# Hybrid decoder layer on one core: where the MLP gate is applied, where the last residual is added, and how w2's preparation and w_out's halves are ordered

## Chip, core and metric

The kernel runs as one program on one core of a Trainium2 chip. The metric is the device time of one execution, in microseconds (us), shown as the median of three runs. The engines are named as in the profile: PE (TensorE matmul), DVE (VectorE), ACT (ScalarE), POOL (GpSimd) and SP (SyncE, which issues the DMAs).

## The reference

One decoder layer with 2048 tokens of width 1024 in float32. What matters here is the second half:

```python
y = jnp.concatenate([a, r], axis=-1) @ w_out[l]
x = layer_norm(ALPHA * x + gt1 * y, ln1_g[l], ln1_b[l])

h = x * (1.0 + sc2) + sh2
f = jnp.square(jax.nn.relu(h @ w_ff1[l])) @ w_ff2[l]
x = layer_norm(ALPHA * x + gt2 * f, ln2_g[l], ln2_b[l])
```

`a` and `r` are the results of multi-head latent attention and of retention. `gt1` and `gt2` are rows of 1024 numbers, the same for all tokens, that are computed from the condition vector `c`. `w_ff1` is 1024 x 4096, `w_ff2` is 4096 x 1024, `w_out` is 1024 x 1024. Since `gt2` scales columns, it can be multiplied into `f` or into the columns of `w_ff2`.

## The kernel before

All products are made of float32 operands split into a high part and a rest: `split` (L122 to L129) rounds on ACT (L126) and subtracts on DVE or POOL (L129), and `mm3` (L131 to L134) issues three matmuls. So each operand costs one ACT and one DVE pass before PE can use it, and the third matmul, which needs the low part of the weights, is the one at L134.

The program runs in stages. Up to about 1076 us of the span it does the conditioning, the input projections, retention and attention. Then follow:

- **w_out** (L925 to L1007, about 1076 to 1280 us): token tiles in pairs, 16 in all, in four groups of four (`border`). The columns of w_out are worked in two halves, n=0 and n=1. Raw rows of w_out are multiplied by `gt1` (L954: POOL for half 0, DVE for half 1) and split into `wo`, which lies in the pools `wo0` and `wo1`. For each pair the residual part `axl` is prepared (ACT L985, POOL L986 with the row `ag`, DVE L987 with the row `ab`); `ag` and `ab` are loaded and scaled on POOL first (L959). The sum with the product is normalised (L1000, L1001), stored to `z_d`, transposed on PE (L965), scaled on ACT (L967, `h2f`) and stored as the MLP's input.
- **FFN up** (L1060 to L1185, about 1280 to 1995 us): two halves of the tokens. In each, 16 channels of w_ff1 are worked in pairs with a Winograd-Strassen scheme of seven products per channel (`up`, `prod`), each product being 12 matmuls of 128x512. The weights of a product are combined on POOL (L1080), split into `w1h` (ACT) and `w1l` (DVE), and the seven combinations of the input (`hh`, `hl`) come from `split_h`. The results are squared ReLUs that are stored to `g_d`.
- Beside that, `prep` and `work` prepare w_ff2: 16 units, eight in each half, each with a 1 MB load `w2r` and then seven pieces. A piece subtracts (DVE L1140), splits into one of two buffers `w2s` (ACT L126, DVE L129) and stores to `wt_d` (L1143). The loop at L1151 to L1185 takes pieces from the generator `todo` after each product, at a pace that `slots` and `want` set. In the last quarter of the units (s=3) the raw rows are multiplied by `gt2` first (L1134, two multiplies of 128x1024 a unit).
- **FFN down** (`down`, L1251 to L1334, about 1997 to 2649 us): two halves of the tokens, four steps s each. A step has seven products of 48 matmuls (P1, P5, P6, P3, then P7, P2, P4; in s=3 P2 stands before P7). The operands `gP..h` and `gP..l` are split from `a` (loaded from `g_d`, combined at L1272), the weights `wP` are loaded from `wt_d`. After each product its PSUM tiles are added to `acc` in SBUF (L1304). At s=2, `gate` (L1215) multiplies each quarter of `acc` by `gt2` once that quarter's last product of the step is added, 16 multiplies of 128x512 in each half: what the first three steps add carries no gate yet. At s=3, `residual` (L1220) loads four pieces `zt` from `z_d`, scales them on POOL (L1226, L1227) and adds them on DVE (L1229), for one quarter after each of P1, P5, P6 and P3. `finish` (L1231) normalises and stores.

The order of the instructions on each engine is not written out by hand. The framework's scheduler sets it from the order and the dependences of the program as written; `tc.issue_after(i)` makes it place what is issued inside the block behind instruction `i`. `load_rows` (L1206) loads the four rows that `residual` and `finish` use, after step s=1 of half 0.

The pools of one stage reuse the memory of pools that were closed before, so which tiles a new stage overwrites depends on the order in which the pools were opened.

## Time and profile before

| what | value |
|---|---|
| median of 3 runs | 2664.97 us (2663.29 to 2665.64) |
| profiled execution | 2665.75 us, span 2663.9 us |
| busy PE | 2453.7 us, 92% of the span |
| busy DVE | 1816.5 us, 68% |
| busy ACT | 1202.8 us, 45% |
| busy POOL | 1160.7 us, 44% |

A row of the timeline is: start, duration, engine, line, operation, output<-inputs, shape, count, and in brackets how long the engine had been idle and what released it. A row of the windows is: the stretch and its length, then the busy time of each engine with the number of instructions, the granted TensorE clock as a share of full speed, the DMA engines' busy share, GB/s. A group of instructions ends with busy time, mean duration in ns, idle time before it and its releaser. A row of the waits gives the engine and instruction that waited, what it waited for, and total us, how often, and the longest. Durations of neighbouring instructions on an engine overlap by a few hundredths to a few tenths of a us.

### The profile page before, as it was taken

To read this page: it belongs to the slowest core of one execution; us is meant where nothing else is said; L and a number is where in the kernel's file an instruction comes from. 1 tells how busy PE (TensorE), PEld (TensorE's weight loads), DVE (VectorE), ACT (ScalarE), POOL (GpSimd) and SP (SyncE) were. 2 spreads that over 40 slices of the span, in tenths; PEclk is the share of its full clock that TensorE was granted. 3 is DMA by queue.
4 is the path that set the end of the run, shared out by engine and by line. 5 is a ranking of instruction groups with operands and counts; after the bars stand their busy time and mean duration, and the time that the engine had idled before them with its cause. 6 is when DMAs were issued, how large, how long until landed. Compare 5 with 4: busy or idle time off the path is not lost.

```text
span 2663.9 us, 34047 instructions
## 1 busy us (share of the span) xinstructions
PE 2453.7 (92%) x11668; PEld 2020.8 (76%) x11668; DVE 1816.5 (68%) x2927; ACT 1202.8 (45%) x2349; POOL 1160.7 (44%) x1087
## 2 busy tenths in 40 slices
PE   6999999989999999699799999889999999899996
PEld 5877778877787878588576787767778887778874
DVE  8757675566767676644767757877544568965698
ACT  5653222257777777333546555456552211232111
POOL 4323546557888988433303236323310004730056
PEclk9999999989999999799899999999999999999998
DMA  9466341020202021555488833877538676776553
GB/s 325 144 216 205 112 136 39 32 78 25 64 17 64 22 60 40 177 177 202 154 283 295 285 124 119 274 261 272 193 137 320 243 277 233 282 291 245 207 209 138
DMA packets 205773, 464.71 MB, mean 174 GB/s; under 512 B 18840, under 2 KB 53016, under 8 KB 191264
## 3 DMA queue, kind: packets, MB, share of 16 engines
q1 hardware_dynamic: 205600, 462.54, 49.9%
q8 instruction: 92, 1.51, 0.2%
q14 instruction: 81, 0.66, 0.1%
HBM read 313.30 MB, written 149.17 MB: 174 GB/s over the span
## 4 chain that ended last, share of the span: by engine, by line
PE 58%; DVE 16%; DMA 13%; issue 5%; ACT 5%; POOL 3%; SPq 1%; DVEq 0%; ACTq 0%; POOLq 0%
DMA wt_d<-w2s 6%; PE t L835 3%; PE d_W L134 3%; PE d_W L132 3%; PE d_W L133 3%; DMA wad<-in_w_ada 2%; PE psY L133 2%; PE psY L134 2%; PE psY L132 2%; PE pj L134 2%; PE pj L132 2%; PE o L826 2%; PE pj L133 2%; PE o L828 2%; PE s L132 2%
## 5 line engine op out<-in xcount | busy, mean ns | idle before, releaser
L1080 POOL TENSOR_TENSOR w<-w,w 128x512 f32<-128x512 f32 x112 | 166.8, 1495 | 385.5 <-DMA w<-in_w_ff 225.4
L129 DVE TENSOR_TENSOR w1l_P<-w,w1h_P 128x512 fp32r<-128x512 f32 x224 | 202.6, 907 | 76.0 <-ACT w1h_P L126 75.3
L807 ACT ACTIVATE p<-s,nm 128x512 f32<-128x512 f32 (+3 forms) x320 | 196.6, 627 | 42.6 <-DVE nm L804 39.1
L802 DVE TENSOR_REDUCE mx<-s 128x1 f32<-128x512 f32 (+3 forms) x288 | 175.2, 621 | 56.5 <-PE s L134 53.7
L1226 POOL TENSOR_TENSOR zt<-zt,ag 128x512 f32<-128x512 f32 x32 | 52.5, 1652 | 307.2 <-DMA zt<-z_d 307.2
L851 POOL TENSOR_TENSOR tl<-tf,th 128x512 fp32r<-128x512 f32 x144 | 183.6, 1287 | 1.7
L835 PE MATMUL t<-ident,p 128*128 128x128 f32 x1088 | 165.5, 277 | 7.3 <-DVE tl L129 3.2
L126 ACT ACTIVATE w1h_P<-w 128x512 fp32r<-128x512 f32 x224 | 136.9, 620 | 74.1 <-PE u_Y L133 23.2
L835 PEld LDWEIGHTS t<-ident,p 128*128 128x128 f32 x1088 | 130.9, 142 | 32.7 <-ACT tf L846 6.4
L133 PE MATMUL pj<-wbl,hhb 128*128 128x512 f32 x384 | 151.4, 395 | 0.7 <-DVE wbl L129 0.7
L132 PE MATMUL pj<-wbh,hhb 128*128 128x512 f32 x384 | 150.7, 395 | 0.9 <-ACT wbh L126 0.6
L134 PE MATMUL pj<-wbh,hlb 128*128 128x512 f32 x384 | 151.4, 395 | 0.0
L129 DVE TENSOR_TENSOR w2s<-w2r,w2s 128x512 fp32r<-128x512 f32 x112 | 95.8, 858 | 73.7 <-ACT w2s L126 73.4
L132 PE MATMUL s<-kt,qt 96*128 96x512 f32 (+3 forms) x320 | 129.5, 405 | 12.3 <-ACT p L807 10.2
L126 ACT ACTIVATE w2s<-w2r 128x512 fp32r<-128x512 f32 x112 | 70.3, 629 | 150.3 <-DMA wt_d<-w2s 137.2
L826 PE MATMUL o<-th,v 128*128 128x512 f32 (+2 forms) x320 | 123.6, 391 | 5.0 <-DVE osum L862 4.2
L828 PE MATMUL o<-tl,v 128*128 128x512 f32 (+2 forms) x320 | 124.5, 398 | 3.3 <-DVE tl L129 1.8
L133 PE MATMUL s<-kt,qt 96*128 96x512 f32 (+3 forms) x320 | 119.9, 375 | 3.7 <-DVE kt L129 3.7
L134 PE MATMUL s<-kt,qt 96*128 96x512 f32 (+3 forms) x320 | 119.7, 375 | 0.0
L132 PE MATMUL psY<-wo_h,mh 128*128 128x512 f32 x256 | 101.4, 402 | 18.8 <-ACT wo_h L126 18.3
L134 PE MATMUL u_Z<-hh_P,w1l_P 128*128 128x512 f32 x256 | 102.9, 402 | 14.9 <-DVE w1l_P L129 14.9
L134 PE MATMUL u_X<-hh_P,w1l_P 128*128 128x512 f32 x256 | 102.8, 402 | 10.8 <-DVE w1l_P L129 10.6
(376 smaller groups left out, 7739.5 us busy)
## 6 DMA issues: line engine op xcount, KB each, us to landing
wP<-wt_d SPq DMA_DIRECT2D x112, 1024.0 KB, 5.0
wt_d<-w2s SPq DMA_DIRECT2D x112, 512.0 KB, 4.2
w<-in_w_ff SPq DMA_DIRECT2D x128, 256.0 KB, 3.5
a<-g_d SPq DMA_DIRECT2D x32, 1024.0 KB, 6.0
g_d<-v SPq DMA_DIRECT2D x96, 256.0 KB, 3.5
wad<-in_w_ada SPq DMA_DIRECT2D x64, 256.0 KB, 2.9
w2r<-in_w_ff SPq DMA_DIRECT2D x16, 1024.0 KB, 5.5
x<-in_x SPq DMA_DIRECT2D x16, 512.0 KB, 8.1
```

The lines of the kernel that those rows point to most:

```text
L126: A.activation(hi, x, AF.Copy)
L129: lo_eng.tensor_tensor(lo, x, hi.bitcast(F32), op=OP.subtract)
L132: T.matmul(ps, sh, mh, start=start, stop=False, skip_group_check=more)
L133: T.matmul(ps, sh, ml, start=False, stop=False, skip_group_check=more)
L134: T.matmul(ps, sl, mh, start=False, stop=stop, skip_group_check=more)
L802: V.tensor_reduce(mx[:, j:j + 1], ps[:, :n], op=OP.max, axis=AX.X)
L807: A.activation(pt[:, :m], b[:, :m], AF.Exp, bias=nm, accum_out=rs[:, qi, j:j + 1])
L826: T.matmul(po[:, cs], w, th[:, cs], start=(done == 0), stop=False)
L828: T.matmul(po[:, cs], w, tl[:, cs], start=False, stop=(done == nk))
L835: T.transpose(tp[:, qi * P:(qi + 1) * P], pts[h, 4 * qb + qi, kb // 4][1][:, kb % 4 * P:(kb % 4 + 1) * P], ident)
L851: (V if mode == "C" else G).tensor_tensor(tl[:, cs], tf[:, cs], th[:, cs].bitcast(F32), op=OP.subtract)
L1080: (V if half == 0 and c < W1V else G).tensor_tensor(src, *sub, op=op)
```

## The change

1. Every unit of w2 is multiplied by `gt2` before it is split (it was one unit in four). The two multiplies of a unit are now two pieces of their own, so a unit has nine pieces and `want` is 72 in each half. `gate` with its 32 multiplies of `acc` is gone.
2. `residual` adds one quarter in each step, after P6 (it was all four quarters in s=3). `load_rows` is called in the first step of half 0, after P5.
3. The instruction that makes a product's low part `w1l` is kept in the list `lows`, and each piece of w2 is issued behind the latest of them.
4. The pools `wo0` and `wo1` change places, and the last pair of token tiles works half n=1 of w_out before n=0.

```diff
--- before.py
+++ after.py
@@ -58,7 +58,7 @@
 WTB = 21
 WMS = "GV"
 WLS = "VV"
-RES = dict(P1=(0, 1), P5=(1, 1), P6=(0, 0), P3=(1, 0))
+RES = (0, 0), (1, 1), (0, 1), (1, 0)
 WOS = "wwww", "xxzz"
 FB4 = "GVGVGVGV", "GVGVGVGV"
 FM4 = "GGGGGGGG", "GGGGGGGG"
@@ -119,14 +119,18 @@
     dbg = {} if dbg is None else dbg
     V, A, G, T, Q = nc.vector, nc.scalar, nc.gpsimd, nc.tensor, nc.sync
 
-    def split(x, hi, lo, hi_eng=None, lo_eng=None):
+    lows = []
+
+    def split(x, hi, lo, hi_eng=None, lo_eng=None, log=None):
         hi_eng = hi_eng or A
         lo_eng = lo_eng or V
         if hi_eng is A:
             A.activation(hi, x, AF.Copy)
         else:
             hi_eng.tensor_copy(hi, x)
-        lo_eng.tensor_tensor(lo, x, hi.bitcast(F32), op=OP.subtract)
+        i = lo_eng.tensor_tensor(lo, x, hi.bitcast(F32), op=OP.subtract)
+        if log is not None:
+            log.append(i.ins)
 
     def mm3(ps, sh, sl, mh, ml, start, stop, more=False):
         T.matmul(ps, sh, mh, start=start, stop=False, skip_group_check=more)
@@ -928,10 +932,10 @@
     m3 = pool(p3, "m3", 2)
     z3 = pool(p3, "z3", 6)
     wor = pool(p3, "wor", 2)
-    wo1 = pool(p3, "wo1")
+    wo0 = pool(p3, "wo0")
     ax3 = pool(p3, "ax3", 2)
     c3 = pool(p3, "c3")
-    wo0 = pool(p3, "wo0")
+    wo1 = pool(p3, "wo1")
     x3 = pool(p3, "x3", 2)
     ps3 = pool(p3, "ps3", 4, space=PSUM)
     pt3 = pool(p3, "pt3", 4, space=PSUM)
@@ -988,14 +992,14 @@
                 z = z3.tile([P, D], F32, tag="z", name=f"z{tt}")
                 ops.append((tt, mh, ml, ax, z))
                 xns.append(z)
-            for n in range(2):
+            for m, n in enumerate((1, 0) if b == border[-1] and tp == 1 else (0, 1)):
                 cs = slice(n * 512, (n + 1) * 512)
                 for tt, mh, ml, ax, z in ops:
                     ps = ps3.tile([P, 512], F32, tag="mm", name=f"psY{tt}_{n}")
                     for k in range(KD):
                         mm3(ps, mh[:, k, :], ml[:, k, :], *wo[n][k], k == 0, k == KD - 1)
                     V.tensor_tensor(z[:, cs], ps, ax[:, cs], op=OP.add)
-                    if n == 0:
+                    if m == 0:
                         continue
                     rs, nm = ln_stats(sm3, z)
                     A.activation(z, z, AF.Identity, bias=nm, scale=rs)
@@ -1080,7 +1084,7 @@
                 (V if half == 0 and c < W1V else G).tensor_tensor(src, *sub, op=op)
             wh = w1p.tile([P, 512], R32, tag="wh", name=f"w1h{half}_{c}_{name}")
             wl = w1p.tile([P, 512], R32, tag="wl", name=f"w1l{half}_{c}_{name}")
-            split(src, wh, wl, A, V)
+            split(src, wh, wl, A, V, lows)
             hh, hl = H[name]
             for k in range(4):
                 ks = slice(k * P, (k + 1) * P)
@@ -1129,9 +1133,8 @@
         s, k = divmod(u, 4)
         b = hraw.tile([P, 2, D], F32, tag="raw", name=f"w2r{u}")
         Q.dma_start(b, I["w_ff2"][8 * s * P:(8 * s + 8) * P].rearrange("(i k p) c -> k p i c", i=2, p=P)[k])
-        if s == NST - 1:
-            for i in range(2):
-                V.tensor_tensor(b[:, i], b[:, i], gt2, op=OP.mult)
+        for i in range(2):
+            V.tensor_tensor(b[:, i], b[:, i], gt2, op=OP.mult)
             yield
         b11, b12, b21, b22 = (b[:, i, 512 * j:512 * j + 512] for i in range(2) for j in range(2))
         for x, (src, sub) in enumerate(((b11, None), (b12, (b12, b11)), (b12, (b22, b12)), (b22, None), (b21, None),
@@ -1154,7 +1157,7 @@
         todo = work(range(8 * half, 8 * half + 8))
         slots = [i for i in range(7 * NCH) if half or i < 7 * NCH - 8]
         slots = slots[14:-10] if half else slots[12:]
-        want = 8 * 7 + 4 * half
+        want = 8 * 9
         count = 0
         Hn = {}
         nxt = split_h(1, Hn) if half == 0 else None
@@ -1168,7 +1171,8 @@
                     i = 7 * c + 2 * x + y
                     if i in slots:
                         while count < min(want, -(-(slots.index(i) + 1) * want // len(slots))):
-                            next(todo, None)
+                            with tc.issue_after(lows[-1]):
+                                next(todo, None)
                             count += 1
                 if nxt is not None and c == NCH - 2:
                     next(nxt, None)
@@ -1211,11 +1215,6 @@
 
     def quarter(half, i, tp, j):
         return acc[4 * i + tp][:, 512 * j:512 * j + 512]
-
-    def gate(half, i, j):
-        for tp in range(4):
-            c = quarter(half, i, tp, j)
-            V.tensor_tensor(c, c, gt2[:, 512 * j:512 * j + 512], op=OP.mult)
 
     def residual(half, i, j):
         cs = slice(512 * j, 512 * j + 512)
@@ -1302,10 +1301,10 @@
                         A.activation(c, ps[ch, tp], AF.Copy)
                     else:
                         V.tensor_tensor(c, c, ps[ch, tp], op=OP.add)
-                if s == NST - 2 and (name, i, j) in (("P2", 0, 0), ("P3", 0, 1), ("P7", 1, 1), ("P4", 1, 0)):
-                    gate(half, i, j)
-            if last and name in RES:
-                residual(half, *RES[name])
+            if half == 0 and s == 0 and name == "P5":
+                load_rows()
+            if name == "P6":
+                residual(half, *RES[s])
 
         sub, plus = OP.subtract, OP.add
         load_a(0, 0)
@@ -1336,8 +1335,6 @@
     for half in range(2):
         for s in range(NST):
             down(half, s, half * NST + s)
-            if half == 0 and s == 1:
-                load_rows()
     p4.close()
     ctx.close()
 
```

Three places show how the order of instructions moves. Numbers at the end of names are tile numbers, which differ between the two kernels by themselves.

**POOL at the end of attention and the start of w_out.** `th` and `tl` are attention's transposed probabilities, `wo_0` raw rows of w_out's half 0. Before:

```order
681 L850 TENSOR_SCALAR th<-tf 128x512 x2
682 L851 TENSOR_TENSOR tl<-tf,th 128x512 x2
683 L867 COPY rc<-ri_11089 128x4x64
684 L867 COPY rc<-ri_12759 128x4x64
685 L959 TENSOR_SCALAR ag_13253<-ag_13253 128x1024
686 L986 TENSOR_TENSOR axl_13265<-axl_13265,ag_13253 128x1024
687 L986 TENSOR_TENSOR axl_13277<-axl_13277,ag_13253 128x1024
688 L959 TENSOR_SCALAR ab_13254<-ab_13254 128x1024
689 L954 TENSOR_TENSOR wo_0_13171<-wo_0_13171,gt_5754 128x512
690 L954 TENSOR_TENSOR wo_0_13172<-wo_0_13172,gt_5754 128x512
```

With the change:

```order
679 L958 TENSOR_TENSOR wo_0_13171<-wo_0_13171,gt_5754 128x512
680 L958 TENSOR_TENSOR wo_0_13172<-wo_0_13172,gt_5754 128x512
681 L854 TENSOR_SCALAR th<-tf 128x512 x3
682 L855 TENSOR_TENSOR tl<-tf,th 128x512 x3
683 L958 TENSOR_TENSOR wo_0_13181<-wo_0_13181,gt_5754 128x512
684 L871 COPY rc<-ri_11089 128x4x64
685 L871 COPY rc<-ri_12759 128x4x64
686 L958 TENSOR_TENSOR wo_0_13182<-wo_0_13182,gt_5754 128x512
687 L958 TENSOR_TENSOR wo_0_13191<-wo_0_13191,gt_5754 128x512
688 L963 TENSOR_SCALAR ag_13253<-ag_13253 128x1024
689 L990 TENSOR_TENSOR axl_13265<-axl_13265,ag_13253 128x1024
690 L990 TENSOR_TENSOR axl_13277<-axl_13277,ag_13253 128x1024
```

Five multiplies of `wo_0` by `gt1` stand ahead of `ag` and `axl` now, three of them among operations of attention. Before, these followed behind both (the first two are shown).

**DVE in the second half of FFN up.** A stretch with a unit's two multiplies by `gt2`. Before:

```order
2099 L129 TENSOR_TENSOR w1l_5_P_18516<-w_1_5_10_18281,w1h_5_P_18515 128x512
2100 L129 TENSOR_TENSOR w2s_1_19021<-w2r_18937,w2s_1_19021 128x512
2101 L1140 TENSOR_TENSOR w2r_18937<-w2r_18937 128x512
2102 L1112 TENSOR_TENSOR v_5_18437<-v_5_18437,u_5_W 128x512
2103 L1140 TENSOR_TENSOR w2r_18937<-w2r_18937 128x512
2104 L1134 TENSOR_TENSOR w2r_19798<-w2r_19798,gt_14754 128x1024 x2
2105 L129 TENSOR_TENSOR w1l_4_P_18536<-w_1_4_11_18251,w1h_4_P_18535 128x512
2106 L1140 TENSOR_TENSOR w2r_19798<-w2r_19798 128x512
2107 L129 TENSOR_TENSOR w1l_5_P_18566<-w_1_5_11_18283,w1h_5_P_18565 128x512
2108 L129 TENSOR_TENSOR w2s_2_19045<-w2r_18937,w2s_2_19045 128x512
```

With the change:

```order
2219 L131 TENSOR_TENSOR w1l_10_P_19545<-w_1_10_10_19304,w1h_10_P_19544 128x512
2220 L1137 TENSOR_TENSOR w2r_19564<-w2r_19564,gt_14754 128x1024
2221 L1113 TENSOR_TENSOR v_11_19491<-u_11_19404,u_11_Z 128x512
2222 L1116 TENSOR_TENSOR v_10_19468<-v_10_19468,u_10_W 128x512
2223 L131 TENSOR_TENSOR w1l_11_P_19569<-w_1_11_10_19333,w1h_11_P_19568 128x512
2224 L1137 TENSOR_TENSOR w2r_19564<-w2r_19564,gt_14754 128x1024
2225 L1116 TENSOR_TENSOR v_11_19491<-v_11_19491,u_11_W 128x512
2226 L131 TENSOR_TENSOR w1l_10_P_19590<-w_1_10_11_19306,w1h_10_P_19589 128x512
2227 L131 TENSOR_TENSOR w2s_0_19615<-w2r_19564,w2s_0_19615 128x512
2228 L131 TENSOR_TENSOR w1l_11_P_19620<-w_1_11_11_19335,w1h_11_P_19619 128x512
2229 L1143 TENSOR_TENSOR w2r_19564<-w2r_19564 128x512
```

The two multiplies stood together (x2) between pieces of another unit, ahead of the low part of the next product. Now each stands by itself, directly behind a low part `w1l`, and so do the pieces of the split `w2s` and of L1143.

**DVE in the last down step (s=3) of the first half of the tokens, around the low part of P5.** `acc` are the accumulators, `d_2_W` and `d_3_W` PSUM tiles of the steps s=2 and s=3. Before:

```order
2417 L1229 TENSOR_TENSOR acc_3_20447<-acc_3_20447,zt_013_21918 128x512
2418 L1304 TENSOR_TENSOR acc_6_20519<-acc_6_20519,d_2_W_21345 128x512
2419 L1218 TENSOR_TENSOR acc_4_20515<-acc_4_20515,gt_14754 128x512
2420 L1304 TENSOR_TENSOR acc_7_20521<-acc_7_20521,d_2_W_21346 128x512
2421 L1218 TENSOR_TENSOR acc_5_20517<-acc_5_20517,gt_14754 128x512
2422 L129 TENSOR_TENSOR gP5l_3_0_21931<-a_0_3_10_21828,gP5h_3_0_21930 128x1024
2423 L1218 TENSOR_TENSOR acc_6_20519<-acc_6_20519,gt_14754 128x512
2424 L1218 TENSOR_TENSOR acc_7_20521<-acc_7_20521,gt_14754 128x512
2425 L1272 TENSOR_TENSOR a_0_3_10_21828<-a_0_3_10_21828,a_0_3_00_21827 128x1024
2426 L129 TENSOR_TENSOR gP5l_3_1_21962<-a_0_3_10_21828,gP5h_3_1_21961 128x1024
2427 L1272 TENSOR_TENSOR a_0_3_00_21827<-a_0_3_11_21829,a_0_3_10_21828 128x1024
```

With the change:

```order
2446 L131 TENSOR_TENSOR gP1l_3_1_21940<-a_0_3_00_21895,gP1h_3_1_21939 128x1024
2447 L1303 TENSOR_TENSOR acc_4_20539<-acc_4_20539,d_2_W_21407 128x512
2448 L1303 TENSOR_TENSOR acc_5_20541<-acc_5_20541,d_2_W_21408 128x512
2449 L1303 TENSOR_TENSOR acc_6_20543<-acc_6_20543,d_2_W_21409 128x512
2450 L1303 TENSOR_TENSOR acc_7_20545<-acc_7_20545,d_2_W_21410 128x512
2451 L131 TENSOR_TENSOR gP5l_3_0_21979<-a_0_3_10_21896,gP5h_3_0_21978 128x1024
2452 L1271 TENSOR_TENSOR a_0_3_10_21896<-a_0_3_10_21896,a_0_3_00_21895 128x1024
2453 L1271 TENSOR_TENSOR a_0_3_00_21895<-a_0_3_11_21897,a_0_3_10_21896 128x1024
2454 L131 TENSOR_TENSOR gP5l_3_1_22010<-a_0_3_10_21896,gP5h_3_1_22009 128x1024
2455 L1271 TENSOR_TENSOR a_0_3_10_21896<-a_0_3_10_21896,a_0_3_00_21895 128x1024
```

The gate's multiplies (L1218) and the residual's adds (L1229) that stood among the last sums of step s=2 and ahead of `gP5l_3_0` and `gP5l_3_1` are gone from there.

## Rows read from the trace of the kernel before

**Rows 1.** The page's head and its part 1 (busy us, share, instructions).

```profile
span 2663.9 us, 34047 instructions
PE 2453.7 (92%) x11668; PEld 2020.8 (76%) x11668; DVE 1816.5 (68%) x2927; ACT 1202.8 (45%) x2349; POOL 1160.7 (44%) x1087
```

**Rows 2.** Windows, by stage; columns as explained above.

```profile
1270.00:1350.00 80.00, 55.78 (x229) 43.16 (x228) 55.85 (x60) 41.94 (x58) 24.95 (x12) 0.83 0.53 185
1360.00:1520.00 160.00, 147.44 (x622) 114.54 (x621) 121.56 (x162) 88.17 (x161) 40.06 (x25) 1.00 0.85 284
1660.00:1860.00 200.00, 178.72 (x743) 140.92 (x743) 160.27 (x200) 112.06 (x200) 67.45 (x40) 0.97 0.78 268
2000.00:2100.00 100.00, 100.00 (x439) 82.66 (x439) 52.60 (x53) 28.26 (x35) 0.00 (x0) 0.99 0.75 278
2226.00:2260.00 34.00, 28.21 (x116) 22.56 (x115) 33.97 (x27) 5.26 (x5) 20.77 (x12) 0.95 0.50 188
2260.00:2315.00 55.00, 47.67 (x200) 38.91 (x199) 51.22 (x60) 13.21 (x13) 42.30 (x29) 0.91 0.74 268
```

**Rows 3.** Timeline of POOL, DVE and PE at the start of w_out.

```profile
1088.72 4.68 POOL L986 TENSOR_TENSOR axl<-axl,ag 128x1024 f32<-128x1024 f32 x2
...
1094.45 3.42 DVE L987 TENSOR_TENSOR axl<-axl,ab 128x1024 f32<-128x1024 f32 x2 [6.71 <-POOL ab L959]
1099.46 2.48 DVE L954 TENSOR_TENSOR wo<-wo,gt 128x512 f32<-128x512 f32 x4
...
1085.36 1.22 PE L132 MATMUL psY<-wo_h,mh 128*128 128x512 f32 x2 [8.71 <-ACT wo_h L126]
...
1100.86 1.22 PE L132 MATMUL psY<-wo_h,mh 128*128 128x512 f32 x2 [9.62 <-ACT wo_h L126]
```

**Rows 4.** Timeline of ACT and PE as the up stage starts.

```profile
1347.41 0.63 ACT L126 ACTIVATE w2s<-w2r 128x512 fp32r<-128x512 f32 x1 [6.62 <-DMA wt_d<-w2s]
1348.47 0.58 ACT L1102 ACTIVATE u<-u_X 128x512 f32<-128x512 f32 x1
...
1349.10 0.80 PE L132 MATMUL u_X<-hh_P,w1h_P 128*128 128x512 f32 x1 [4.67 <-ACT u L1102]
1349.69 0.63 PE L133 MATMUL u_X<-hl_P,w1h_P 128*128 128x512 f32 x1
```

**Rows 5.** PE's waits, 1620 to 1960 us (second half of up).

```profile
PE u_Y L134 <- DVE w1l_P L129: 8.6, 4, 3.8
PE u_X L134 <- DVE w1l_P L129: 8.1, 7, 2.8
PE u_Z L134 <- DVE w1l_P L129: 6.8, 4, 4.3
```

**Rows 6.** A gate pair in up: timeline of DVE and PE; the line's durations.

```profile
1759.04 4.53 DVE L1134 TENSOR_TENSOR w2r<-w2r,gt 128x1024 f32<-128x1024 f32 x2
...
1765.43 0.50 PE L134 MATMUL u_Y<-hh_P,w1l_P 128*128 128x512 f32 x1 [3.84 <-DVE w1l_P L129]
...
L1134 DVE TENSOR_TENSOR w2r<-w2r,gt x8: 1217/1225/2315, 1701.6 to 1787.8; 128x1024 f32<-128x1024 f32 x8
```

**Rows 7.** PE's waits, 1960 to 2360 us (down, first half, and what follows).

```profile
PE d_X L132 <- issue: 7.3, 1, 7.3
PE d_Z L134 <- DVE gP5l L129: 4.9, 1, 4.9
```

**Rows 8.** PE's waits, 2360 to 2664 us (down, second half).

```profile
PE d_X L132 <- issue: 8.6, 1, 8.6
PE d_Z L134 <- DVE gP5l L129: 2.7, 2, 2.1
```

**Rows 9.** Groups of DVE instructions by line.

```profile
L1229 DVE TENSOR_TENSOR acc<-acc,zt 128x512 f32<-128x512 f32 x32 | 43.6, 1376 | 3.5 <-POOL zt L1227 3.5
L1304 DVE TENSOR_TENSOR acc<-acc,d_Z 128x512 f32<-128x512 f32 x56 | 37.6, 684 | 7.9 <-PE d_Z L134 7.8
L1218 DVE TENSOR_TENSOR acc<-acc,gt 128x512 f32<-128x512 f32 x32 | 31.8, 1000 | 0.0
```

## The prediction

> **What bounds the kernel now.** The page's head comes first: PE is busy 92% of a span of 2663.9 us, and no other engine comes near it [rows 1]. So time can only be won where PE stands idle, and the question for each part of the change is which idle stretch it touches. The windows, stage by stage, show where those are. In a down step that nothing disturbs, PE is busy in all of 100 us, 0.2278 us for each of 439 matmuls, with DVE at 52.60 [rows 2]. There, other engines' work costs nothing. It is lost in six other places: 24.2 of 80 us as the up stage starts, 12.6 of 160 in up's first half, 21.3 of 200 in its second, and 5.8 of 34 and 7.3 of 55 us in the last down step of the first half [rows 2]; and the timeline shows two gaps at the start of w_out [rows 3]. In up's second half every large wait is for `w1l`, the low part that DVE makes [rows 5]: DVE is busy there 160.27 of 200 us [rows 2], and what counts is what stands in its queue ahead of the low part. So the order on DVE matters more than its total.
>
> My sum is made against the profiled execution, 2665.75 us, which is 0.8 above the median of 2664.97. A measurement of this kernel can tell some 0.2% (5 us) from no change.
>
> **A. The start of w_out.** PE waits 8.71 us for the first piece of w_out, does 12 matmuls in all, and then waits 9.62 us until 1100.86 [rows 3]. What it waits for the second time is a queue on DVE: two `axl` sums that end at 1097.87, then multiplies of half 1 by `gt1` from 1099.46 [rows 3]; the sums in turn wait for POOL's `axl` (from 1088.72) and `ab`. With the change POOL multiplies most of half 0 ahead of that, and in PE's new order 44 matmuls of half 0 stand ahead of the first one of half 1, which still comes about 1100.9, and four more soon after it; 12 stood there before. 36 matmuls at 0.2278 are 8.2 us that move into an idle stretch. Against that, POOL gets multiplies between attention's last operations; I charge 2 us. **-6.** Ends: -14, if the first gap shrinks as well (most of 8.71 gone); +3, if the multiplies hold up attention's tail and the gap at 1100 stays.
>
> **B. The start of up.** As up starts, ACT holds the split of a w2 piece that waits 6.62 us for a `w2s` buffer to be stored; the copy of `u` stands behind it, and PE waits 4.67 us for that copy [rows 4]. The matmul after it takes 0.63 us and not what it takes undisturbed: the granted clock is low after an idle. In the change's order no w2 piece stands on ACT or DVE in this stretch: the first unit begins at the 15th low part, not the 7th. So 4.7 us of wait and some 1.5 us of clock go: **-6.** Behind it the next input combination (`hh`) may be late, so the ends are 0 and -12 (half of the 24.2 us of idle).
>
> **C. The w2 pieces in up.** Before, the units filled the first part of each half and left none at its end, hence 12.6 + 21.3 = 33.9 us of idle in these two windows, and another 6 us in the second by its granted clock of 0.97 over 200 us [rows 2]: 40. Now they are spread evenly (each half ends with pieces in nearly the last slot), and each stands directly behind a low part, so a low part finds at most the pieces between it and the one before. Half of the waits is what I take to go: **-20.** Nearest rows for the ends: nothing goes, 0; all of it, -40, as in the down step at 52.60 of 100, where PE never waits.
>
> **D. The gate moved.** Of the 32 multiplies of `acc`, 31.8 us on DVE [rows 9], none is left; in exchange 12 units more are multiplied in up, 24 multiplies of 128x1024. A multiply takes 1.217 to 2.315 us [rows 6], so this is 29 to 56 us more for DVE in a stage where it is the limit. Cover: DVE has a fifth of its time free even in the worst window [rows 2]. If the cover is gone, the price shows in the one pair of before that came out badly: two multiplies back to back, 4.53 us, and PE waits 3.84 us for the low part behind them [rows 6]. In the change the two stand apart, each behind a low part, and a product on PE lasts 12 x 0.2278 = 2.7 us, about one multiply at its longest. I charge 0.5 us for each of the 12 units: **+6**; ends 0 and 24 (2 us a unit).
>
> **E. The last down steps.** In the first half, P5 waits 4.9 us for its low part `gP5l` and P2 waits 7.3 us ("issue", that is for PSUM tiles that DVE has yet to read) [rows 7]; in the second half the same waits are 2.7 and 8.6 [rows 8]. Both come from what DVE has in front: 16 adds of `zt` at a mean of 1376 ns in each half and, just before P5, the gate's multiplies [rows 9]. DVE is busy 33.97 of 34 us there [rows 2]. With the change only one group of four adds falls in the step, around P6's low part, and no multiply. P5's waits go to nearly 0; P2 must still wait for the sums after P3, up to four of 0.68 us [rows 9], of which some overlap PE: I leave 2.3. First half: 4.9 + 5.0, and 1.7 for the clock (0.95 over 34 us [rows 2]): -12. Second half: 2.2 + 6.3 and 1.5 of clock: -10. What is added: the other three groups go into steps where DVE had half its time free, at no cost, except where the second half's first step meets `finish` of the first half: +3. The four rows and the first `zt` now load in the first step, about 3 MB among 278 GB/s at a DMA share of 0.75 [rows 2]; they stand in SP's queue ahead of the next weights `wP`: +2. **-17**, ends -26 and -8. After the last matmul nothing changes: the last sums, the norm and the store.
>
> The part of w_out's change that swaps the halves of the last pair moves no matmul's count, and I cost it at nothing of its own; its effect on memory is inside B.
>
> **Sum:** -6 - 6 - 20 + 6 - 17 = -43, so 2665.75 - 43 - 0.8 = **2622 us**.
>
> **A rule that speaks against it.** On DVE, the 56 sums with an input in PSUM have a mean of 684 ns, those beside POOL's scalings among them, while the adds of `zt`, with both inputs in SBUF, have one of 1376 [rows 9], and the same multiply takes 1.217 or 2.315 us [rows 6]. The Trainium skill, page "SBUF — State Buffer", section "Who interferes with whom", says why: a DVE instruction with two SBUF inputs and a GpSimd instruction that reads SBUF lock each other out, and the later one waits for the whole of the earlier. The durations here agree. By that rule spreading `zt` saves none of the contention, it only moves it. What that would make of the sum is the first rival, worked out from the rows.
>
> **Rivals.**
> - *Contention moves with the residual.* POOL's 8 scalings of a group now run in six steps that had none. There a DVE instruction with two SBUF inputs can take 0.7 to 1.1 us longer. If each of these six steps then loses 2.5 us at a low part, close to the 2.7 of P5 in the second half [rows 8], E falls from -17 to -2 and the time is 2637. For it: the doubled durations. Against: DVE has 47 us free in 100 there [rows 2].
> - *Spreading doesn't help in up.* If pieces cost PE what they cost now wherever they stand, C is 0, and with the multiplies at 6 the sum is -23: 2642. For it: `w2s` has two buffers, so a late store stops ACT and DVE in any order [rows 4]. Against: the waits are for low parts, and these are what the order now favours.
> - *All waits in up go.* C is -40 and D 0: 2622 - 20 - 6 = 2596.
> - *Slower: the multiplies make DVE the bound of up.* DVE's share in the second half is 0.80 with only four units multiplied. If each of the 12 new units costs what the bad pair cost, 3.84 us of wait [rows 6] and some 1 us of clock, that is 58 us, and if with DVE so full the order wins nothing (C is 0), then A, B and E (-29) leave 2665 + 58 - 29 = 2694; it is slower than before as soon as a unit costs over 2.4 us. It decides at the point where a low part and what stands between two low parts take DVE longer than the 2.7 us that PE works on a product: a multiply of 2.3 and a sum of 0.68 with the low part's 0.69 are over it, a multiply of 1.22 is not. So it depends on how often POOL is busy at that moment: 67.45 of 200 us [rows 2], a third.
> - *The change doesn't do what it says*, because the scheduler places the pieces elsewhere: the order on the engines shows them where they should be, so this has next to no chance.
>
> **How the numbers follow.** Forecast (2607 to 2634): 0.50. Spreading doesn't help: 0.17, contention moves: 0.10, both near 2640. All waits go: 0.13. DVE bound: 0.10, of which some 0.03 end within 0.2%, where a unit costs about 2.4 us. The range leaves out DVE as the bound and the far ends of the rest. Below it reaches to "all waits go" with A at -10 as well, 2592; above to "spreading doesn't help" with B at 0 and A at -2, 2652. Faster 0.89, same 0.04, slower 0.07.
>
> **What would show it.** A: over 40 matmuls of `psY` before 1100 us. B: no wait of PE for `u` behind `w2s`. C and D: in the two windows of up, PE idle halved, and waits for `w1l` none above 2 us; if D failed, L1137 at 2.3 us ahead of each such wait. E: from 2226 us on, waits for `gP5l` under 1 us and for d_X under 3; if contention moves, new waits at `gP3l` or `gP6l` in steps 0 to 2. The forecast is wrong if PE's idle time in up doesn't fall, or if steps 0 to 2 grow beyond 336 x 0.2278 = 76.5 us.

## The result

The changed kernel takes 2602.32 us (median of 4 runs, 2601.14 to 2603.63) against 2664.13 for the one before (2662.37 to 2665.64): the ratio is 0.9768, with a 95% interval of 0.9751 to 0.9785. The forecast was 2622 us with a range of 2592 to 2652. The direction and the range held; the gain is 62 us where 43 were forecast, and the time lies below the main case of 2607 to 2634.

The page of the changed kernel: the span and the busy time of the engines.

```profile
span 2600.1 us, 34036 instructions
...
PE 2438.0 (94%) x11668; PEld 2019.8 (78%) x11668; DVE 1822.7 (70%) x2919; ACT 1200.0 (46%) x2349; POOL 1175.3 (45%) x1087
```

PE's busy share rose from 92 to 94%, while DVE does slightly more than before (1822.7 us against 1816.5 in [rows 1]). So the gain does not come from less work on DVE; most of the same work stands in another place. PE's own busy time fell by 15.7 us for the same 11668 matmuls: in three of the windows below the granted clock is 1.00 where it was 0.97, 0.95 and 0.91, so part of the gain does not show as idle time.

The windows of the changed kernel that answer to [rows 2], moved to where the same stages now lie:

```profile
1265.00:1345.00 80.00, 61.28 (x245) 47.17 (x245) 51.76 (x54) 39.96 (x56) 26.29 (x13) 0.83 0.43 148
1345.00:1505.00 160.00, 160.00 (x707) 132.49 (x706) 130.76 (x172) 92.26 (x164) 40.51 (x25) 1.00 0.75 255
1640.00:1840.00 200.00, 197.95 (x869) 162.25 (x868) 157.80 (x198) 117.94 (x209) 76.03 (x45) 1.00 0.72 242
1960.00:2060.00 100.00, 100.00 (x442) 82.79 (x442) 62.95 (x58) 27.83 (x34) 30.10 (x18) 1.00 0.84 318
2186.00:2220.00 34.00, 34.00 (x151) 28.15 (x151) 29.56 (x30) 7.23 (x7) 13.90 (x8) 1.00 0.60 219
2220.00:2275.00 55.00, 54.67 (x241) 44.94 (x241) 44.76 (x62) 18.25 (x19) 27.81 (x20) 1.00 0.81 307
```

At the start of up PE's idle time fell from 24.2 to 18.7 of 80 us. In up's first half 12.6 us of 160 became none, in the second 21.3 of 200 became 2.0, though DVE is as busy there as before (157.80 us against 160.27). That is the main reading: DVE's total did not set these waits. (Not all of the first half gained: its last 336 matmuls, where the pieces now run beside the preparation of the second half's inputs, take 90.0 us and not 78.1.) In the last down step of the first half, 5.8 and 7.3 us became 0 and 0.3.

PE's largest waits from 1600 to 1950 us, the end of up's first half and all of its second, answer to [rows 5]; the three largest rows summed to 23.5 us and now sum to 10.2, of which 8.2 lie ahead of 1650 us, at the border between the halves:

```profile
PE u_Z L138 <- DVE w1l_P L131: 4.2, 4, 1.5
PE u_X L138 <- DVE w1l_P L131: 3.3, 2, 2.7
PE u_W L138 <- DVE w1l_P L131: 2.7, 1, 2.7
```

The start of w_out (timeline of POOL, DVE and PE), against [rows 3], and a wait of PE at the start of up that the profile puts to a w2 piece:

```profile
1075.71 1.29 POOL L958 TENSOR_TENSOR wo<-wo,gt 128x512 f32<-128x512 f32 x1
1089.14 5.15 POOL L990 TENSOR_TENSOR axl<-axl,ag 128x1024 f32<-128x1024 f32 x2
...
1095.34 3.41 DVE L991 TENSOR_TENSOR axl<-axl,ab 128x1024 f32<-128x1024 f32 x2 [3.25 <-POOL ab L963]
...
1080.38 0.50 PE L136 MATMUL psY<-wo_h,mh 128*128 128x512 f32 x1 [1.30 <-ACT mh L128]
...
1097.25 1.22 PE L136 MATMUL psY<-wo_h,mh 128*128 128x512 f32 x2 [4.95 <-ACT wo_h L128]
...
1101.88 1.22 PE L136 MATMUL psY<-wo_h,mh 128*128 128x512 f32 x2 [3.40 <-ACT wo_h L128]
...
1340.35 0.47 PE L136 MATMUL u_Z<-hh_P,w1h_P 128*128 128x512 f32 x1 [2.90 <-ACT w2s L128]
```

POOL starts six of half 0's eight multiplies before attention's last matmul; before, two. PE starts after 1.30 us and not after 8.71, and 44 matmuls of `psY` start before 1100 us, where 12 did. It then waits 4.95 and 3.40 us and not 9.62; the chain over POOL's `axl` and DVE's sums hardly moved. And the waits in down, 1940 to 2300 us, against [rows 7]:

```profile
PE d_W L136 <- DMA wP<-wt_d: 8.1, 1, 8.1
PE d_W L138 <- DVE gP6l L131: 5.0, 2, 3.4
```

The waits for `gP5l` (4.9) and for PSUM (7.3) are gone, but a new one stands at the first matmul of down: 8.1 us for the first weights. From 2300 us on, against [rows 8]:

```profile
PE d_W L136 <- issue: 4.5, 1, 4.5
PE d_Z L138 <- DVE gP3l L131: 2.0, 2, 1.0
```

The waits for `gP5l` (2.7) and for PSUM ahead of P2 (8.6) are gone here too. The 4.5 us stand ahead of the last product, P4 of s=3, where the kernel before waited 3.4.

**Time by stage.** Each column is the time from the first matmul of a stage to the first of the next in PE's timeline (w_out: from the end of attention's last matmul; "up to down": from up's last matmul to down's first; last step: to its last matmul). The second half's steps 1 and 2, left out, take 152.3 us together in all fourteen kernels. The table is the yardstick of everything below, because the end of attention, ahead of all of this, falls anywhere between 1070.2 and 1081.1 us in the profiled executions, which moves totals but not stages. Each row is one profiled execution.

| kernel (median of its runs, us) | w_out | up, 1st half | up, 2nd half | up to down | down, steps 0-2 | step 3 | 2nd half, step 0 | last step |
|---|---|---|---|---|---|---|---|---|
| before (2664) | 211.9 | 364.1 | 341.6 | 3.2 | 230.2 | 94.2 | 78.3 | 96.4 |
| the change (2602) | 200.8 | 357.1 | 310.2 | 8.5 | 230.2 | 76.2 | 86.6 | 83.5 |
| no queueing (2635) | 200.7 | 367.8 | 343.3 | 3.1 | 228.6 | 76.2 | 86.9 | 82.0 |
| only queueing (2617) | 211.4 | 343.8 | 309.2 | 9.3 | 230.2 | 93.8 | 78.3 | 95.0 |
| no gate (2589) | 201.4 | 347.6 | 307.6 | 8.1 | 231.4 | 76.2 | 86.6 | 82.3 |
| gate twice (2614) | 201.5 | 361.6 | 319.5 | 9.3 | 230.1 | 76.2 | 86.7 | 83.4 |
| gate on POOL (2639) | 201.9 | 379.4 | 329.6 | 8.4 | 230.5 | 76.2 | 86.9 | 83.5 |
| residual as before (2612) | 200.8 | 353.9 | 307.9 | 8.3 | 231.1 | 88.4 | 78.4 | 88.0 |
| residual group late (2593) | 201.7 | 355.4 | 309.6 | 8.5 | 230.2 | 76.2 | 79.3 | 82.2 |
| pools as before (2605) | 212.1 | 348.8 | 311.3 | 8.8 | 231.3 | 76.2 | 86.6 | 82.3 |
| slots early (2601) | 202.2 | 354.9 | 317.3 | 3.1 | 230.2 | 76.2 | 86.6 | 82.3 |
| late group, a behind low part (2582) | 200.6 | 356.2 | 309.4 | 3.1 | 230.1 | 76.2 | 79.2 | 82.1 |
| gate in half the units (2586) | 201.8 | 345.1 | 311.2 | 8.3 | 231.1 | 78.4 | 79.3 | 83.2 |
| both (2576) | 201.2 | 344.2 | 309.8 | 3.0 | 228.6 | 78.2 | 79.3 | 83.1 |

Where the change alters nothing in a stage, the stage repeats within 1 or 2 us; up's first half varies more, 353.9 to 357.1 in four kernels that don't differ there (348.8 in one more).

### The profile page after: what moved, and what is told of

Its sections match the earlier page's. It is cut to its first block, busy times and chain, and to the rows that moved or that the text cites. A ratio compares the mean times of both kernels' runs of the same rounds, so it can differ in the third digit from the quotient of the medians.

```text
span 2600.1 us, 34036 instructions
## 1 busy us (share of the span) xinstructions
PE 2438.0 (94%) x11668; PEld 2019.8 (78%) x11668; DVE 1822.7 (70%) x2919; ACT 1200.0 (46%) x2349; POOL 1175.3 (45%) x1087
## 4 chain that ended last, share of the span: by engine, by line
PE 58%; DVE 15%; DMA 12%; issue 6%; ACT 6%; POOL 3%; SPq 0%; DVEq 0%; ACTq 0%; POOLq 0%
PE d_W L136 4%; PE d_W L137 4%; PE d_W L138 4%; PE t L839 3%; DMA wad<-in_w_ada 2%; DVE w1l_P L131 2%; DMA g_d<-r 2%; DMA wt_d<-w2s 2%; PE pj L138 2%; PE pj L136 2%; PE pj L137 2%; PE o L830 2%; PE d_Z L138 2%; PE o L832 2%; PE d_Z L136 2%
## 5 line engine op out<-in xcount | busy, mean ns | idle before, releaser
L1084 POOL TENSOR_TENSOR w<-w,w 128x512 f32<-128x512 f32 x112 | 182.0, 1634 | 346.9 <-DMA w<-in_w_ff 242.9
L1271 DVE TENSOR_TENSOR a<-a,a 128x1024 f32<-128x1024 f32 x64 | 97.3, 1532 | 24.0 <-DMA a<-g_d 22.8
L131 DVE TENSOR_TENSOR tl<-t,th 128x512 fp32r<-128x512 f32 (+3 forms) x176 | 92.3, 538 | 24.0 <-ACT th L128 22.7
```

The lines of the kernel that those rows point to most:

```text
L131: i = lo_eng.tensor_tensor(lo, x, hi.bitcast(F32), op=OP.subtract)
L1084: (V if half == 0 and c < W1V else G).tensor_tensor(src, *sub, op=op)
```

## The experiments

**1. The queueing, taken away and put in alone.** Theory 1: what gains in up is where a piece of w2 stands, behind a low part. Theory 2: it is the pace, nine small pieces in place of seven. First, away from the changed kernel:

```diff
-                            with tc.issue_after(lows[-1]):
-                                next(todo, None)
+                            next(todo, None)
```

> The changed kernel with w2's pieces no longer issued behind the low parts; all else as changed. Theory 1 (the place behind the low part is what gains in FFN up): the units bunch up again in the first part of each half, the start of up and its second half lose their gains of 8.5 and 31 us, and the extra multiplies now stand in a full DVE queue: 2640 to 2660 us. Theory 2 (the gain comes from the pace alone, nine small pieces instead of seven, with the gate in pieces of their own): 2597 to 2607 us.

Measured: 2635.0 us, 5 us below theory 1's range. Up takes 711.0 us against 705.7 before and 667.2 with the change: all of the gain in up is gone, and 5 us more, while w_out and down keep theirs. PE's waits in up, 1340 to 1990 us:

```profile
PE u_Z L138 <- DVE w1l_P L131: 12.8, 6, 8.2
PE u_Z L136 <- ACT w1h_P L128: 7.9, 3, 3.0
PE u_Y L138 <- DVE w1l_P L131: 7.4, 7, 2.2
```

Then alone, in the kernel before (`lows`, `log` and `issue_after` as in the change, nothing else):

> The kernel before with one part of the change alone: w2's pieces issued behind the latest low part. Theory 1: the start of up and its second half gain what they gained with the whole change (8.5 and 31 us), up to 5 us are given back where down starts and waits for its first weights, w_out and the last down steps stay as before: 2625 to 2635 us. Theory 2: no change, 2658 to 2668 us.

Measured: 2617.33 us, more than either theory gave. Up takes 652.9 us, 52.7 less than before and 14 less than with the whole change. The same waits, 1320 to 1940 us:

```profile
PE u_Z L138 <- DVE w1l_P L131: 3.3, 3, 1.6
PE u_Z L136 <- DVE v L1113: 3.0, 2, 1.6
PE u_X L138 <- DVE w1l_P L131: 2.3, 1, 2.3
```

These two kernels differ in more than the queueing, so each is set beside the kernel that it was made from. The row for low parts of `u_Z` over all of up: before and with only the queueing, then with the change and without its queueing:

```profile
PE u_Z L134 <- DVE w1l_P L129: 14.9, 11, 4.3
PE u_Z L138 <- DVE w1l_P L131: 6.3, 4, 3.0
...
PE u_Z L138 <- DVE w1l_P L131: 6.3, 5, 2.1
PE u_Z L138 <- DVE w1l_P L131: 16.0, 7, 8.2
```

Over all tiles of up, PE's waits for low parts go from 38.1 to 10.8 us in the first pair, and from 17.9 to 35.2 in the second. Theory 2 falls: without the queueing the nine pieces gain nothing. Left to itself, the scheduler places the pieces early: in the order on DVE, without the queueing, the subtractions and splits of the first eight units stand between low parts 8 and 68 of 112, with it between 15 and 104.

**2. The price of the gate in up.** The multiply left out, then made twice:

```diff
-            V.tensor_tensor(b[:, i], b[:, i], gt2, op=OP.mult)
```

> The changed kernel with w2's 32 multiplies by the gate row left out (the MLP is added without its gate); pieces, pace and queueing unchanged. Theory 1 (the 24 added multiplies cost 14 us, all in the first half of up, as the comparison with the kernel that only queues the pieces suggests): up takes 653 us in place of 667, the first half alone 343 in place of 357: 2586 to 2592 us. Theory 2 (the multiplies are covered, and the nine pieces and their pace make that difference): up stays at 664 to 668 us, 2598 to 2604 us.

```diff
             V.tensor_tensor(b[:, i], b[:, i], gt2, op=OP.mult)
+            V.tensor_tensor(b[:, i], b[:, i], gt2, op=OP.mult)
```

> The changed kernel with each multiply of w2 by the gate row made twice (the output then carries the square of the gate): 32 more multiplies of 128x1024, 39 to 74 us of DVE time in up. The price of the prediction (0.5 us a unit): 16 units, +8, 2610 us. Theory that the multiplies are covered: below +3, 2600 to 2605 us. Theory that DVE becomes the bound (3.84 us a unit): +61, 2663 us.

Measured: 2588.99 and 2614.17 us. Without the 32 multiplies up takes 655.2 us, 12.0 less; with 32 more 681.1, 13.9 more; the totals move by 13.3 and 11.9. So a multiply costs about 0.4 us of PE's time. Without them the first half, where 16 of them are new, falls by 9.5 us, the second by 2.6; but the first half varies by some us between kernels that don't differ there, and with 32 more it is the second half that grows most (9.3 of the 13.9), so how the price divides between the halves is not shown. Theory 1 of the first run holds in its total, both rivals of the second fall, and the price that the prediction set (0.25 us a multiply) came out too low in both runs.

**3. The gate on POOL**, which is busy less than half of the time:

```diff
-            V.tensor_tensor(b[:, i], b[:, i], gt2, op=OP.mult)
+            G.tensor_tensor(b[:, i], b[:, i], gt2, op=OP.mult)
```

> The changed kernel with w2's multiplies by the gate row on POOL in place of DVE. Theory 1 (what costs is DVE's time, 32 multiplies of 1.2 to 2.3 us): FFN up falls from 667 us towards the 653 us that it takes with 24 multiplies fewer: 2588 to 2595 us. Theory 2 (two SBUF inputs on both engines lock each other out, so DVE loses the same time waiting): up stays at 665 to 680 us, 2600 to 2615 us.

Measured: 2639.32 us, and up 709.0: up is as slow as before the change, worse than theory 2 had it. Groups of instructions, first with the change, then with the gate on POOL (there with the page's line of busy times):

```profile
L131 DVE TENSOR_TENSOR w1l_P<-w,w1h_P 128x512 fp32r<-128x512 f32 x224 | 206.8, 929 | 76.0 <-ACT w1h_P L128 73.8 <-DMA w<-in_w_ff 1.6
L1137 DVE TENSOR_TENSOR w2r<-w2r,gt 128x1024 f32<-128x1024 f32 x32 | 43.3, 1355 | 0.0
```

```profile
PE 2453.4 (93%) x11668; PEld 2024.4 (77%) x11668; DVE 1824.8 (69%) x2887; ACT 1198.1 (45%) x2349; POOL 1255.3 (48%) x1119
...
L131 DVE TENSOR_TENSOR w1l_P<-w,w1h_P 128x512 fp32r<-128x512 f32 x224 | 229.7, 1032 | 99.1 <-ACT w1h_P L128 97.0 <-DMA w<-in_w_ff 1.6
...
L1137 POOL TENSOR_TENSOR w2r<-w2r,gt 128x1024 f32<-128x1024 f32 x32 | 84.6, 2663 | 95.2 <-DMA w2r<-in_w_ff 95.2
```

A multiply takes 2663 ns on POOL and 1355 on DVE, and DVE's low parts grow from a mean of 929 to 1032 ns. DVE was relieved of 43.3 us of multiplies, but its busy time is 1824.8 us and was 1822.7: what stayed on it takes some 45 us longer, 23 of them in the low parts, as theory 2 had it. The Trainium skill, page "SBUF — State Buffer", section "Who interferes with whom", states that a DVE instruction with two SBUF inputs contends with a GpSimd instruction that reads SBUF; the longer low parts agree with it, and so do w2's subtractions (L1143), which go from 851 to 989 ns, while the sums that read PSUM (L1113) keep theirs, 679 and 680 ns. So DVE's load stayed and up still grew by 41.8 us on PE. The low parts also come later: DVE stands idle 99.1 us ahead of them, mostly for `w1h`, and stood 76.0; PE's waits for low parts grow from 17.9 to 32.2 us, those for `w1h` itself from 0.3 to 7.6. That points at w1's combinations, which now share POOL's queue with the multiplies; it was not tried apart.

**4. The residual back in the last step**, and the rows loaded as before:

```diff
-RES = (0, 0), (1, 1), (0, 1), (1, 0)
+RES = dict(P1=(0, 1), P5=(1, 1), P6=(0, 0), P3=(1, 0))
...
-            if half == 0 and s == 0 and name == "P5":
-                load_rows()
-            if name == "P6":
-                residual(half, *RES[s])
+            if last and name in RES:
+                residual(half, *RES[name])
```

> The changed kernel with the residual back in the last step (four quarters after P1, P5, P6 and P3) and the rows loaded after the second step, as before. Theory A (the residual's adds made the waits of the last steps): the last steps of both halves lose their gains of 18 and 13 us, the 8 us lost in the second half's first step come back: about +23, 2620 to 2630 us. Theory B (the gate's multiplies of the accumulators made them): the last steps keep most, and the 8 us come back: 2592 to 2602 us.

Measured: 2612.05 us, between the two theories; down, from its first to its last matmul, takes 638.2 us, between 628.9 with the change and 649.7 with only the queueing, which still has both. So it is both: the multiplies out of `acc` give 11.5 us, the residual's place another 9.3, after it has paid 8.2 in the second half's first step. The wait for PSUM before P2 is the residual's alone; here it is back in both halves (2170 to 2600 us):

```profile
PE d_X L136 <- issue: 15.8, 2, 8.5
```

**5. One residual group of the second half a step later.** In the changed kernel the second half's first step takes 86.6 us, and not 78.3. POOL, DVE and PE there (timeline):

```profile
2294.53 3.36 POOL L1247 TENSOR_TENSOR acc<-acc,g 128x1024 f32<-128x1024 f32 x1
...
2291.70 1.75 DVE L1228 TENSOR_TENSOR acc<-acc,zt 128x512 f32<-128x512 f32 x1 [2.45 <-POOL zt L1226]
2293.38 2.28 DVE L131 TENSOR_TENSOR gP6l<-a,gP6h 128x1024 fp32r<-128x1024 f32 x1
...
2295.71 0.50 PE L138 MATMUL d_W<-wP,gP6l 128*128 128x512 f32 x1 [3.42 <-DVE gP6l L131]
```

PE waits for `gP6l`, which takes DVE 2.28 us, behind an add of `zt` that waits 2.45 us for POOL; and POOL has the norm of the first half (L1247) between its scalings.

```diff
-            if name == "P6":
+            if name == "P6" and (half == 0 or s):
                 residual(half, *RES[s])
+            if name == "P7" and half == 1 and s == 1:
+                residual(half, *RES[0])
```

> The changed kernel with one group of residual adds moved in the second half of the tokens: out of its first step (after P6), into its second (after P7). Theory 1 (in the first step the adds meet the norm of the first half on POOL and DVE): that step falls from 86.6 us to about 78.4, as in the kernel before, and no other grows: 2594 us. Theory 2 (the norm alone makes these waits): the step stays at 85 to 87 us, no change.

Measured: 2592.92 us. The step takes 79.3 us, and the next ones don't grow; of its waits this is left (2255 to 2345 us):

```profile
PE d_Z L138 <- DVE gP3l L131: 1.3, 1, 1.3
PE d_W L138 <- DVE gP6l L131: 0.6, 1, 0.6
```

Theory 1 holds; 152.3 us for the second half's steps 1 and 2, one of which took the group, are unchanged.

**6. The pools of w_out's halves in their old places**, with the last pair's order as changed:

```diff
-    wo0 = pool(p3, "wo0")
+    wo1 = pool(p3, "wo1")
     ax3 = pool(p3, "ax3", 2)
     c3 = pool(p3, "c3")
-    wo1 = pool(p3, "wo1")
+    wo0 = pool(p3, "wo0")
```

> The changed kernel with the pools wo0 and wo1 back in their old places (the last pair still works half 1 first). Theory 1 (the place in memory decides when half 0's rows can be multiplied and split): the second gap of PE at the start of w_out returns in full, w_out ends 8 to 9 us later: about 2611 us. Theory 2 (the order of the last pair, or the scheduler's other moves, gave it): under 2 us, 2601 to 2604 us.

Measured: 2604.92 us (2597.34 to 2608.44), a total that tells nothing, since attention ended 9 us earlier in its profiled run than with the change. The stage does tell: 212.1 us, as before the change (211.9), against 200.8. Theory 1 holds for the stage, but not for the gap that it named: PE's waits there are 8.74, 5.74 and 3.30 us, so it is the first gap of the kernel before (8.71) that is back. The order of the last pair was not tried alone.

**7. The new wait at the start of down.** Timeline of DVE, SP and PE in the changed kernel:

```profile
1919.26 5.15 DVE L131 TENSOR_TENSOR w1l_P<-w,w1h_P 128x512 fp32r<-128x512 f32 x4 [0.56 <-ACT w1h_P L128]
1930.46 2.36 DVE L1271 TENSOR_TENSOR a<-a,a 128x1024 f32<-128x1024 f32 x2 [6.05 <-DMA a<-g_d]
...
1947.69 0.33 SPq L1100 DMA_DIRECT2D g_d<-v  x1
1948.07 2.43 SPq L1269 DMA_DIRECT2D wP<-wt_d  x4
...
1955.61 0.77 PE L136 MATMUL d_W<-wP,gP1h 128*128 128x512 f32 x1 [8.09 <-DMA wP<-wt_d]
```

DVE has the first combination of `a` (L1271) in its queue ahead of up's last sums and waits 6.05 us there for the load of `a`; the results of up that ACT and SP still have to store are late by that, and SP issues the first weights `wP` behind one of those stores, at 1948.07, after up's last matmul (1947.13). In the kernel before it issued them 5 us ahead of that. Two edits, first w2's last pieces earlier:

```diff
-        slots = [i for i in range(7 * NCH) if half or i < 7 * NCH - 8]
-        slots = slots[14:-10] if half else slots[12:]
+        slots = [i for i in range(7 * NCH) if half or i < 7 * NCH - 20]
+        slots = slots[14:-22] if half else slots[12:]
```

> The changed kernel with w2's pieces in the slots up to 12 earlier at the end of each half. Theory 1 (the last pieces hold the memory and the DMA queue that down's first operands and the second half's inputs need): the 8.5 us between the last matmul of up and the first of down fall to about 3, and the last quarter of the first half of up falls from 90 us towards 80: 2588 to 2595 us. Theory 2 (pieces packed closer cost as much as the late ones): 2600 to 2606 us.

Measured: 2601.31 us, no change, and both theories have a part: up to down falls to 3.1 us, but the second half of up, packed closer, grows by 7.1, and the last 336 matmuls of its first half take 86.9 us and not the 80 of theory 1. Then, in the kernel of experiment 5, the combination held back on DVE:

```diff
                 for dst, y, z, op in subs:
-                    V.tensor_tensor(dst[:, ks], y[:, ks], z[:, ks], op=op)
+                    if n == 0:
+                        with tc.issue_after(lows[-1]):
+                            V.tensor_tensor(dst[:, ks], y[:, ks], z[:, ks], op=op)
+                    else:
+                        V.tensor_tensor(dst[:, ks], y[:, ks], z[:, ks], op=op)
```

> The kernel that adds one residual group of the second half a step later (2593 us), and besides: the combinations of down's first operands in its first step are issued behind the last low part of up, so that DVE doesn't wait for their load ahead of up's last work. Theory 1 (that wait holds up up's last results and with them the issue of down's first weights): PE's wait of 8.1 us at the start of down falls to about 3, the 8.5 us between up and down to 3 or 4: 2586 to 2589 us. Theory 2 (the load itself is late, wherever DVE waits for it): 8 us stay, 2591 to 2595 us.

Measured: 2581.73 us. The same places:

```profile
1929.19 2.35 DVE L1273 TENSOR_TENSOR a<-a,a 128x1024 f32<-128x1024 f32 x2
...
1936.01 6.30 SPq L1269 DMA_DIRECT2D wP<-wt_d  x4
...
1944.40 0.77 PE L136 MATMUL d_W<-wP,gP1h 128*128 128x512 f32 x1 [2.69 <-ACT v L1099]
```

The combination starts without a wait, `wP` is issued 5 us before up's last matmul, and up to down takes 3.1 us. Theory 1 holds for the stage. The total falls by more than it was given: of the 11 us against experiment 5, 5.4 are this stage; in the profiled executions the rest lies ahead of w_out, where attention ended 5.4 us earlier, and the edit is not shown to have caused that.

**8. The gate where it is cheapest.** If the multiplies cost mostly in up's first half, as the run without them has it, they belong in the second alone. So only the units of s=2 and s=3 are multiplied in w2; `acc` is multiplied at the end of s=1, and the residual is added in s=2 and s=3, so that the second half's first step has no adds:

```diff
-RES = (0, 0), (1, 1), (0, 1), (1, 0)
+RES = {(2, "P6"): (0, 0), (2, "P7"): (0, 1), (3, "P1"): (1, 1), (3, "P6"): (1, 0)}
...
-        for i in range(2):
-            V.tensor_tensor(b[:, i], b[:, i], gt2, op=OP.mult)
-            yield
+        if s >= NST - 2:
+            for i in range(2):
+                V.tensor_tensor(b[:, i], b[:, i], gt2, op=OP.mult)
+                yield
...
+                if s == NST - 3 and (name, i, j) in (("P2", 0, 0), ("P3", 0, 1), ("P7", 1, 1), ("P4", 1, 0)):
+                    gate(half, i, j)
```

> The changed kernel with the gate in w2's operands in the second half of its units alone (steps s=2 and s=3); the accumulators are multiplied at the end of s=1, and the residual is added in s=2 (after P6 and P7) and s=3 (after P1 and P6). If the added multiplies cost only in up's first half: that half falls from 357 to about 344 us. In down, the first step of the second half no longer has adds (-8), while two times 16 multiplies on the accumulators come back, at the end of a step that has half of DVE free: 0 to 5 us a time, and two groups in s=3 again: 0 to 5 a time. Sum -21 to 0: 2581 to 2602 us, most likely 2590. If multiplies of the accumulators are what made the last steps slow: 12 us lost behind s=1 in both halves: over 2600 us.

Measured: 2586.24 us. Up's first half falls to 345.1 us, the second half's first step to 79.3; the multiplies of `acc` in s=1 cost at most 0.9 us in the first half and nothing in the second, the two groups in s=3 cost 2.2 us in the first half and nothing in the second. With the edit of experiment 7 on top:

> The two last edits together: gate in w2's operands for the second half of the units alone with the residual in s=2 and s=3, and the combinations of down's first operands issued behind the last low part of up. If they add up, up takes 656 us, up to down 3 us, down 624 us: 5 us less than the first alone (2586) and 4 to 5 less than the second alone (2582): 2576 to 2582 us. If the second one gained by something in the first half of up: 2584 to 2588 us.

Measured: 2576.44 us (5 runs, 2574.36 to 2579.74), ratio to the kernel before 0.9681 (0.9667 to 0.9694). That is faster than each edit alone, and inside the range for edits that add up.

## Why the prediction was right, and where it was not

The mechanisms of C and E were right, those of A and B in part, and the sign of D. The sum of -43 was 20 us short (the spans differ by 63.8): up, where B, C and D were to give -20, gave -38.4; A and E gave 5 to 6 more each; and 5.3 were given back at a place that the prediction did not look at. The time came out between the main case and "all waits in up go", with all of C, as in that rival, and a D that was not 0 but about twice its term.

- **A, -6.** Measured -11.1 (211.9 to 200.8). The count of matmuls ahead of 1100 us was right (44). But the term took its gain out of the second gap, and that one kept 8.35 of 9.62 us; the gain came out of the first gap, 8.71 to 1.30, which the term held for its good end alone. The charge of 2 us for attention's tail can't be seen in what attention's end varies by anyway.
- **B, -6.** The first 336 matmuls of up took 116.9 us and now take 108.4, -8.5, but the number is luck in part. The wait of 4.67 us for `u` is gone; 2.90 us at nearly the same place, which the profile puts to the split of a w2 piece, have come in its stead. The larger part lies at the transposes of w_out's last tiles, where two waits of 4.3 and 4.9 us became two of 1.6; waits for `hh` and `hl`, which the term feared, took some 4 us of that back. Of the two, the 4.3 us for `z` stay with the queueing alone and are gone with the whole change, so another part of the change has a hand in it. The prediction put the new order of the last pair, which touches these tiles, at nothing; it was not tried alone.
- **C, -20.** The queueing alone gave -52.7 in up, of which 11.0 at its start (the first 336 matmuls took 105.9 us with it); the other 41.7 are C without D. The step that failed is "half of the waits is what I take to go": in the windows nearly all of them went (33.9 us to 2.0). The bound from below, -40, was worked out right, and the argument next to it, that a low part finds at most the pieces between it and the one before, had no reason in it for only half.
- **D, +6.** About +10 for 24 new multiplies at 0.4 us each; against "only queueing", which has no nine pieces either, +14. The 32 multiplies keep DVE busy for 43.3 us and cost PE 12 to 14, so some two thirds are covered, as it said in kind. The rival in which DVE becomes the bound fell: not even 32 more multiplies cost 3.84 us a unit.
- **E, -17.** Down as a whole gave -22.6: -18.0 and -12.9 in the last steps (forecast -12 and -10), +8.3 in the second half's first step (forecast +3), nothing in the first half's steps (forecast +2). The first half's term counted the clock of one window (0.95 over 34 us) and left out that of the next (0.91 over 55 us [rows 2], another 5 us). By the prediction's own sign, that steps 0 to 2 don't grow beyond 76.5 us, the second half's first step, at 86.6, went wrong. The rival "contention moves with the residual" fell there: 230.2 us before and after, with 30 us of POOL in 100. It came true only where `finish` runs too.
- **Not in the sum: +5.3 between up and down.** The prediction looked for what the spread pieces do to DVE and not for what stands at the end of the stage that they now reach.

So moving the gate, by itself, gave nothing: 10 to 14 us lost in up, 11.5 won in down, by these sums. It was the condition for spreading the residual, which may be added only to what needs no later gate.

## What to carry to other kernels

What stands in an engine's queue ahead of the one instruction that the bottleneck waits for can count for more than the engine's load: here 53 us of up against the 12 that all 32 multiplies cost. Put background work directly behind that instruction, and look at the waits, not at the busy share. Background work that is spread to the end of a stage meets the first loads of the next one there, so check the seam. An engine that looks idle (POOL here) is no free place for work that slows the busy one down.

## What the runs showed of the hardware

Much of what totals scatter by comes from one stage: attention's last matmul ends between 1070.2 and 1081.1 us in profiled executions of kernels whose edits lie behind it for the most part, while the second half's steps 1 and 2, which have no long waits, take 152.3 us together in every one of them. Differences of 5 us are better read from stages than from medians of four. And moving work to POOL can leave DVE as busy as it was: the gate moved from DVE to POOL took 43.3 us of instructions off the one and put 84.6 on the other, DVE's busy time rose by 2.1 us, and up took 41.8 us longer.
